# Ten of 31 depthwise-convolution taps as ScalarE products that GpSimd's transfers add up in DRAM, and one sum of weight blocks by such a transfer, in a one-core decoder-block kernel

## The chip, the cores and the metric

The kernel runs on one core of one Trainium2 chip. The metric is the device time of one execution in microseconds; lower is better. The kernel before takes 1759.72 us, the median of three runs that lie between 1759.67 and 1759.94 us.

## The reference: what is computed

One decoder block with DEPTH 1, batch 1, 1024 positions of width 1024, all in float32. Cut to what matters here:

```python
h = rms_norm(x, norm_mix_g) * (1 + sc1) + sh1                 # sh1, sc1, g1, sh2, sc2, g2 from c @ w_ada + b_ada
glu_in, qk_in, v, o_pre, if_pre, merge_pre = split(h @ w_in + b_in)
a = glu_in[..., :1024] * sigmoid(glu_in[..., 1024:])
a = causal_depthwise_conv(a, conv_dw_w, conv_dw_b)            # 31 taps: y[t] = sum_j w[j] a[t-30+j] + b, per channel
y_conv = silu(layer_norm(a)) @ w_conv_pw + b_conv_pw
q, k = split(silu(causal_depthwise_conv(qk_in, qk_conv_w, qk_conv_b)))   # 4 taps
hm = mlstm(q, k, v, gates from if_pre)                        # 4 heads of width 256, recurrent over chunks
y_mlstm = sigmoid(o_pre) * group_norm(hm)
x = x + g1 * ((sigmoid(merge_c) * y_conv + sigmoid(merge_m) * y_mlstm) @ w_out)
gt, up = split((rms_norm(x, norm_ffn_g) * (1 + sc2) + sh2) @ w_ffn_up)   # 2 x 2816 columns
out = rms_norm(x + g2 * ((silu(gt) * up) @ w_ffn_down))
```

The change touches two places: the 31-tap convolution of `a`, and the sums of blocks of `w_ffn_up` in the up projection.

## The kernel before, in words

**Numbers.** A float32 product is made of three passes of TensorE over rounded parts: high times high, high times low, low times high. So each 512 KB block of weights (tile `wraw`, 128 x 1024) is split by one ScalarE activation (`whi`, L149) and one VectorE subtraction (`wlo`, L150); `wraw`, `whi` and `wlo` have two buffers each, and the split of a block therefore waits until TensorE has done with the block before the last.

**Stages.** A prologue normalises and transposes x. Then comes the long stage that this text calls the mixing stage, from about 67 to 817 us: the input projection `w_in` in blocks of 128 columns (`wblock`, 48 matmuls of 128 x 512 at L159 and about 11 us each), with the four heads of the mLSTM between them (`mlstm`; its query, key and value blocks at L500 to L563, its recurrent steps at L593 to L690). Layer norm over the convolution, the pointwise convolution, w_out, the up projection, the down projection and the final norm follow. Activations lie with channels on partitions, 1024 positions along the free axis; eight channel tiles `ct` of 128 channels make up the width.

**The 31-tap convolution.** For each channel tile, `glu(ct)` computes two blocks; `glu_gate` makes the sigmoid (L364), `glu_post` writes tile `a` (128 x 1054, with 30 zeros in front; three buffers) and appends 31 steps to a list `bg`. Step 0 is a ScalarE activation that begins the sum `cacc` (L338), steps 1 to 30 are VectorE scalar_tensor_tensor operations on it (L340), 128 x 1024 each. After step 30 a transfer on SyncE's queue stores `cacc` in `conv_d[ct]` in DRAM. Each block of `w_in` takes steps from the list (`pump`): a block brings a credit of PUMP = 5500 and each step costs TAP = 1200, so between four and five taps go beside one block. `go` writes straight into the tile `cv` of the later layer norm where that exists already (`late["cv"]`). Behind the heads, `reload_conv()` loads all stored tiles back on SyncE's queue.

**The order of instructions.** The program is written in the order of those lists, and a list scheduler with a model of time then puts each engine's instructions into a fixed order. On the chip each engine runs its own order, one after the other, and an instruction whose wait is not yet over holds all that stand behind it.

**The up projection.** It multiplies 2 x 2 blocks by seven products instead of eight. For each of the 22 tiles f of 128 columns, `up_sums` loads the gate block g and the up block u (512 KB each, two queue entries on SyncE's queue) and makes three VectorE sums and differences of their halves (128 x 512 each): s3 (L1003), u's first half plus its second half, in place (L1004), two more (L1005, L1006). ScalarE and VectorE then split the results (L994, L995) and `up_run` does the seven products (L1054 to L1056). `up_park` does the sums of the first two tiles ahead, while w_out runs.

Of the kernel before, what the change touches and what calls it, by code (L numbers as in the profile page):

```python
# [8 lines left out]
F32 = mybir.dt.float32  # L9
F32R = mybir.dt.float32r  # L10
I32 = mybir.dt.int32
AF = mybir.ActivationFunctionType
OP = mybir.AluOpType
AX = mybir.AxisListType

S = 1024
# [4 lines left out]
FT = FF // 128  # L21
EPS = 1e-6
TAPS = 31
PUMP = 5500
TAP = 1200
LATER = 500
# [23 lines left out]
def hybrid_block(ctx: ExitStack, tc: tile.TileContext, x, c, w_ada, b_ada, norm_mix_g, w_in, b_in,  # L50
                 conv_dw_w, conv_dw_b, conv_ln_g, conv_ln_b, w_conv_pw, b_conv_pw, qk_conv_w,
                 qk_conv_b, mlstm_norm_g, w_out, norm_ffn_g, w_ffn_up, w_ffn_down, final_norm_g, out):
    nc = tc.nc
# [11 lines left out]
    def ps_mm():  # L65
        return ps.tile([128, 2, 512], F32, name="mm", bufs=2)

    def ps_a():
        return ps.tile([128, 512], F32, name="pa", bufs=1)

    def ps_n():
        return ps.tile([128, 512], F32, name="pn", bufs=1)

    def ps_c():
        return ps.tile([128, 512], F32, name="pc", bufs=2)

    bg = []
# [4 lines left out]
    def pump(ns):  # L82
        credit[0] = min(credit[0] + ns, 1e9) if bg else 0.0
        while bg and credit[0] > 0:
            cost, fn = bg.pop(0)
            at = tc.cur_priority
            tc.cur_priority = at + delay[0]
            fn()
            tc.cur_priority = at
            credit[0] -= cost  # L90
# [52 lines left out]
    def load_split(src, row0, kt, col0, hi=None, lo=None, raw=None, eng=None):  # L143
        if raw is None:
            raw = load_raw(src, row0, kt, col0)
        if hi is None:
            hi = wp.tile([128, kt, 128], F32R, name="whi", tag="whi")
            lo = wp.tile([128, kt, 128], F32R, name="wlo", tag="wlo")
        nc.scalar.activation(hi, raw, AF.Copy)  # L149
        (eng or nc.vector).tensor_sub(lo, raw, hi.bitcast(F32))  # L150
        return hi, lo
# [19 lines left out]
    def flat(t):  # L171
        return t.rearrange("p a b -> p (a b)")
# [41 lines left out]
    def bcol(col0):  # L214
        if col0 < IF0:
            return cols["b_lo"][:, col0 // 128:col0 // 128 + 1]
        i = (col0 - MC0) // 128
        return cols["b_hi"][:, i:i + 1]

    def dw_col(j, ct):  # L220
        r = j * 8 + ct
        return cols["dw0"][:, r:r + 1] if r < 128 else cols["dw1"][:, r - 128:r - 127]
# [3 lines left out]
    for q in range(2):  # L226
# [12 lines left out]
        for k in range(KT):  # L239
            p = ps_n() if k % 3 == 0 else ps_c()  # L240
# [8 lines left out]
    first = [ps_mm(), ps_mm()]  # L249
# [68 lines left out]
    cp = cvp.enter_context(tc.tile_pool(name="cp", bufs=2, side="right", reuse_waits="tile"))  # L318
    hap = ExitStack()
    ha = hap.enter_context(tc.tile_pool(name="ha", bufs=1, side="right", reuse_waits="tile"))  # L320
    hdp = ExitStack()
    hp = hdp.enter_context(tc.tile_pool(name="hp", bufs=1, side="left", reuse_waits="tile"))
    late = {}
# [8 lines left out]
    conv_d = [dram.tile([128, S], F32, name=f"conv_d{i}") for i in range(8)]  # L332
# [3 lines left out]
    def conv_tap(acc, a, j, ct):  # L336
        if j == 0:
            nc.scalar.activation(acc, a[:, 0:S], AF.Identity, scale=dw_col(0, ct), bias=cols["dw_b"][:, ct:ct + 1])  # L338
        else:
            nc.vector.scalar_tensor_tensor(acc, a[:, j:j + S], dw_col(j, ct), acc, op0=OP.mult, op1=OP.add)  # L340

    def glu_post(ct, pa, sg):
        a = cp.tile([128, TAPS - 1 + S], F32, name="a", tag="a", bufs=3)
        nc.gpsimd.memset(a[:, 0:TAPS - 1], 0.0)
        nc.vector.scalar_tensor_tensor(a[:, TAPS - 1:], flat(pa), bcol(ct * 128), sg, op0=OP.add, op1=OP.mult)
        box = []

        def go(j):
            if j == 0:
                if "cv" in late:  # L350
                    box.append(late["cv"](ct))
                else:
                    box.append(cp.tile([128, S], F32, name="cacc", tag="cacc", bufs=2))
            conv_tap(box[0], a, j, ct)
            if j == TAPS - 1 and ct not in cv:
                nc.sync.dma_start(conv_d[ct], box[0])
                done.add(ct)

        for j in range(TAPS):
            bg.append((TAP, lambda j=j: go(j)))  # L360

    def glu_gate(ct, pb):
        sg = tmp4()
        nc.scalar.activation(sg, flat(pb), AF.Sigmoid, bias=bcol(GLU_B + ct * 128))  # L364
        return sg

    cv = {}
    done = set()

    def wblock(col0, busy=PUMP, raw=None):  # L370
        w = load_split(win, 0, KT, col0, raw=raw, eng=WN if raw is not None else None)
        acc = ps_mm()
        for k in range(KT):
            mm_k(acc, k, KT, w, hh, hl)
            pump(busy / KT)
            yield
        return acc
# [138 lines left out]
    def qkv(h):  # L516
# [26 lines left out]
        def v_half(g, ws):  # L543
            acc = ps_mm()
            for i in range(4):
# [4 lines left out]
                for k in range(KT):  # L550
# [3 lines left out]
                    nc.tensor.matmul(o, hh[k][:, ts_], lo[:, k % 4, :], start=False, stop=(k == KT - 1))  # L554
                pump(PUMP / 4)
                yield
# [148 lines left out]

    def merge_conv(e, temp, busy=PUMP):
        pm = yield from wblock(MC0 + e * 128, busy)
        sg = temp()
        with tc.high_priority():
            nc.scalar.activation(sg, flat(pm), AF.Sigmoid, bias=bcol(MC0 + e * 128))  # L710
        nc.scalar.dma_start(mc_d[e], sg)
# [18 lines left out]
    for h in range(NH):  # L730
        box = []
# [17 lines left out]
    def new_cv(ct):  # L749
        cv[ct] = ap_.tile([128, S], F32, name=f"cv{ct}", tag="cv", bufs=8)  # L750
        return cv[ct]

    late["cv"] = new_cv
    def reload_conv():
        for ct in range(8):
            if ct in done and ct not in cv:
                nc.sync.dma_start(new_cv(ct), conv_d[ct])

    reload_conv()

    def t4():
        return ap_.tile([128, S], F32, name="t4b", tag="t4b", bufs=6)
# [118 lines left out]
    p = ps_a()  # L881
# [22 lines left out]
    def k4(name):  # L904
        return up_.tile([128, S], F32, name=name, tag="k4", bufs=2)
# [80 lines left out]
    def weights(kind, name):  # L986
        return wp.tile([128, KT, 128], F32 if kind == "wraw" else F32R, name=name, tag=kind)

    def up_load(f, t, col0):
        nc.sync.dma_start(t, wup[:, col0 + f * 128:col0 + (f + 1) * 128].rearrange("(k p) e -> p k e", p=128))  # L990
        return t

    def split_into(hi, lo, t):
        nc.scalar.activation(hi, t, AF.Copy)  # L994
        nc.vector.tensor_sub(lo, t, hi.bitcast(F32))  # L995
        return hi, lo

    def up_sums(f, gate=True):
        g = up_load(f, weights("wraw", "graw") if gate else k4("graw").rearrange("p (k e) -> p k e", k=KT), 0)
        u = up_load(f, k4("uraw").rearrange("p (k e) -> p k e", k=KT), FF)  # L1000
        gw = split_into(weights("whi", "gh"), weights("wlo", "gl"), g) if gate else None
        s3 = k2("s3").rearrange("p (k e) -> p k e", k=4)
        nc.vector.tensor_sub(s3, g[:, 0:4], u[:, 0:4])  # L1003
        nc.vector.tensor_add(u[:, 0:4], u[:, 0:4], u[:, 4:8])  # L1004
        nc.vector.tensor_sub(g[:, 0:4], u[:, 0:4], g[:, 0:4])  # L1005
        nc.vector.tensor_sub(g[:, 4:8], g[:, 4:8], g[:, 0:4])  # L1006
        return gw, u, g, s3
# [218 lines left out]
    for gidx, nf in enumerate(groups):  # L1226
# [4 lines left out]
        for t in range(8):  # L1231
# [3 lines left out]
            if gidx < 3:  # L1235
                p = ps_mm()
# [40 lines left out]
```

## Time and profile before

| what | value |
| --- | --- |
| three runs | 1759.67, 1759.72, 1759.94 us |
| span of the profiled execution, first to last instruction | 1757.5 us |
| what lies around the span (median less span) | 2.2 us |
| TensorE matmul busy | 1716.9 us, 98% |
| VectorE busy | 1253.3 us, 71% |
| ScalarE busy | 610.9 us, 35% |
| GpSimd busy | 72.9 us, 4% |
| mean granted TensorE clock | 0.994 |
| HBM traffic | 102 GB/s over the span |

All times are microseconds of the one core. PE is TensorE (PEld its weight loads), DVE is VectorE, ACT ScalarE, POOL GpSimd, SP SyncE; L340 is line 340 of the kernel. A row of groups gives line, engine, operation, output and inputs with their shapes, the count, then busy time and mean nanoseconds of one, then how long the engine sat idle just before them and which instruction ended that. A row of the windows gives a stretch of the span and how long each engine was busy in it. A row of the timeline gives start and duration of one instruction, with the idle time before it in brackets. A row of the transfers gives the count, the size of one and the median time from issue to landing. The profiled execution's own time is taken as its span and the 2.2 us around it, 1759.7 us, which is the median of the runs.

### The profile page before, as it was taken

Reading aid. Unit: us, or ns where it says so; the run is one execution under the profiler, and the core shown is the slowest. Engines: PE = TensorE matmul, PEld = TensorE weight load, DVE = VectorE, ACT = ScalarE, POOL = GpSimd, SP = SyncE. Lnnn points to the kernel's source line nnn. Section 1 sums busy time; section 2 is a strip of 40 time slices with the busy share of each in tenths; the row PEclk is TensorE's granted clock in tenths of the full one; section 3 lists DMA queues with packets and bytes.
Section 4 is the critical chain, followed back from the end, with each engine's and each line's share of the span. In section 5 each row is a group of like instructions: output and inputs, shape, how many; then the busy total and the mean of one; then the engine's idle time right before and its main releaser. Section 6 shows DMA issues by size and latency. Waiting matters only on the chain.

```text
span 1757.5 us, 21022 instructions
## 1 busy us (share of the span) xinstructions
PE 1716.9 (98%) x8448; PEld 1436.9 (82%) x8448; DVE 1253.3 (71%) x1652; ACT 610.9 (35%) x791; POOL 72.9 (4%) x121
## 2 busy tenths in 40 slices
PE   5999999999999999999999999999999999999998
PEld 4788888888888888888888788888888888878887
DVE  6888998996689858737689567866666665685243
ACT  6434334322533243223522366423222321232122
POOL 3100001000100000000000000000000000000000
PEclk8999999999999999999999999999999999999999
DMA  9121111111111211224497643322222222653221
GB/s 333 33 60 40 46 60 49 49 60 60 49 37 60 62 46 48 73 60 163 136 374 261 204 156 109 108 84 72 84 84 84 72 85 90 221 168 104 64 89 56
DMA packets 194712, 179.93 MB, mean 102 GB/s; under 512 B 7463, under 2 KB 166711, under 8 KB 194615
## 3 DMA queue, kind: packets, MB, share of 16 engines
q1 hardware_dynamic: 177367, 146.61, 26.8%
q10 hardware_dynamic: 17248, 31.99, 5.0%
q8 instruction: 66, 1.08, 0.3%
q14 instruction: 31, 0.25, 0.0%
HBM read 146.06 MB, written 32.51 MB: 102 GB/s over the span
## 4 chain that ended last, share of the span: by engine, by line
PE 90%; DVE 4%; DMA 3%; issue 1%; ACT 1%; POOL 0%; SPq 0%; POOLq 0%; DVEq 0%; ACTq 0%
PE mm L159 39%; PE mm L1054 5%; PE mm L1055 5%; PE mm L1056 4%; PE mm L552 2%; PE mm L1240 2%; PE mm L1239 2%; PE mm L1241 2%; PE mm L553 2%; PE mm L554 2%; PE pc L1054 1%; DVE macc L268 1%; PE pc L1056 1%; PE pc L1055 1%; PE pa L1056 1%
## 5 line engine op out<-in xcount | busy, mean ns | idle before, releaser
L340 DVE SCALAR_TENSOR_TENSOR cacc<-a,col,cacc 128x1024 f32<-128x1024 f32 x240 | 307.3, 1286 | 4.1 <-ACT cacc L338 1.4
L159 PE MATMUL mm<-hh,whi 128*128 128x512 f32 x864 | 272.8, 392 | 0.8 <-ACT t L364 0.8
L159 PE MATMUL mm<-hl,whi 128*128 128x512 f32 x864 | 271.0, 392 | 0.0
L159 PE MATMUL mm<-hh,wlo 128*128 128x512 f32 x864 | 270.6, 391 | 0.0
L159 PEld LDWEIGHTS mm<-hh,whi 128*128 128x128 f32 x864 | 161.1, 188 | 32.8 <-ACT t L364 1.2
L159 PEld LDWEIGHTS mm<-hh,wlo 128*128 128x128 f32 x864 | 161.3, 188 | 32.3
L159 PEld LDWEIGHTS mm<-hl,whi 128*128 128x128 f32 x864 | 160.5, 188 | 30.9 <-issue 0.2
L149 ACT ACTIVATE whi<-wraw 128x1024 fp32r<-128x1024 f32 x62 | 65.8, 1062 | 228.7 <-PE mm L159 178.5
L150 DVE TENSOR_TENSOR wlo<-wraw,whi 128x1024 fp32r<-128x1024 f32 x60 | 73.2, 1220 | 26.1 <-ACT whi L149 26.0
L552 PE MATMUL mm<-whi,hh 128*128 128x256 f32 x256 | 76.2, 298 | 0.0
L1054 PE MATMUL mm<-Bh,gh 128*128 128x512 f32 (+1 forms) x192 | 71.6, 375 | 1.5 <-ACT gh L994 1.0
L553 PE MATMUL mm<-whi,hl 128*128 128x256 f32 x256 | 72.5, 283 | 0.0
L1055 PE MATMUL mm<-Bl,gh 128*128 128x512 f32 (+1 forms) x192 | 71.5, 373 | 0.6 <-DVE Bl L976 0.6
L554 PE MATMUL mm<-wlo,hh 128*128 128x256 f32 x256 | 71.8, 283 | 0.0
L1056 PE MATMUL mm<-Bh,gl 128*128 128x512 f32 (+1 forms) x192 | 71.2, 372 | 0.0
L505 DVE SCALAR_TENSOR_TENSOR cacc<-qkraw,col,cacc 128x1024 f32<-128x1024 f32 x48 | 61.5, 1280 | 6.7 <-ACT cacc L503 6.0
L1243 DVE TENSOR_TENSOR x<-x,mm 128x1024 f32<-128x1024 f32 x24 | 29.3, 1219 | 51.1 <-PE mm L1241 47.0
L1119 ACT ACTIVATE whi<-wraw 128x512 fp32r<-128x512 f32 (+2 forms) x32 | 25.3, 790 | 110.6 <-PE mm L1241 72.9
L552 PEld LDWEIGHTS mm<-whi,hh 128*128 128x128 f32 x256 | 48.8, 191 | 4.1
L1240 PE MATMUL mm<-fa,wlo 128*128 128x512 f32 x128 | 50.1, 392 | 1.0 <-DVE wlo L1120 0.9
L1239 PE MATMUL mm<-fa,whi 128*128 128x512 f32 x128 | 50.0, 390 | 0.9 <-DVE cu L1082 0.9
L1241 PE MATMUL mm<-fa,whi 128*128 128x512 f32 x128 | 49.9, 390 | 0.0
(442 smaller groups left out, 3898.0 us busy)
## 6 DMA issues: line engine op xcount, KB each, us to landing
wraw<-in_w_in_dram SPq DMA_DIRECT2D x64, 512.0 KB, 4.2
awt<-in_w_ada_dram SPq DMA_DIRECT2D x32, 512.0 KB, 8.1
graw<-in_w_ffn_up_dram SPq DMA_DIRECT2D x24, 512.0 KB, 3.8
uraw<-in_w_ffn_up_dram SPq DMA_DIRECT2D x22, 512.0 KB, 4.7
draw<-in_w_ffn_down_dram SPq DMA_DIRECT2D x22, 512.0 KB, 4.4
act_d<-cg ACTq DMA_DIRECT2D x38, 256.0 KB, 2.2
wad<-in_w_ada_dram SPq DMA_DIRECT2D x16, 512.0 KB, 10.2
wraw<-in_w_out_dram SPq DMA_DIRECT2D x16, 512.0 KB, 4.3
```

The source lines that it names most:

```text
L150: (eng or nc.vector).tensor_sub(lo, raw, hi.bitcast(F32))
L159: nc.tensor.matmul(flat(acc)[:, a:b], lhs[:, k, :], rhs[k][:, a:b], start=(first and k == 0), stop=(last and k == kt - 1))
L340: nc.vector.scalar_tensor_tensor(acc, a[:, j:j + S], dw_col(j, ct), acc, op0=OP.mult, op1=OP.add)
L552: nc.tensor.matmul(o, hh[k][:, ts_], hi[:, k % 4, :], start=False, stop=False)
L553: nc.tensor.matmul(o, hl[k][:, ts_], hi[:, k % 4, :], start=False, stop=False)
L554: nc.tensor.matmul(o, hh[k][:, ts_], lo[:, k % 4, :], start=False, stop=(k == KT - 1))
L1054: nc.tensor.matmul(o, a, rh, start=(k == 0), stop=False)
L1055: nc.tensor.matmul(o, a, rl, start=False, stop=False)
L1056: nc.tensor.matmul(o, b, rh, start=False, stop=(k == 3))
L1239: nc.tensor.matmul(o, hi[:, i, :], his[i][:, a:b], start=(i == 0), stop=False)
L1240: nc.tensor.matmul(o, lo[:, i, :], his[i][:, a:b], start=False, stop=False)
L1241: nc.tensor.matmul(o, hi[:, i, :], los[i][:, a:b], start=False, stop=(i == nf - 1))
```

## The change

Per channel tile, taps 0 to 20 stay as they were (one on ScalarE, 20 on VectorE). Taps 21 to 30 become ScalarE activations that write the product of one tap into a tile `tapp` (two buffers). The first of the ten products is stored in `conv_d[ct]` by a transfer on SyncE's queue; the other nine are added to it there by transfers of GpSimd's queue that add instead of copying (`accum_op`), and so is `cacc` at the end. Each of these ten reads and writes the same 512 KB of DRAM, so each waits for the one before it. Tile `a` has two buffers instead of three. The direct way into `cv` and the first `reload_conv()` are gone; the last one loads all eight tiles. In `up_sums` the addition of L1004 becomes a transfer of GpSimd's queue that adds u's second half to its first in SBUF (256 KB), 22 times.

```diff
+SENT = 10
...
     def glu_post(ct, pa, sg):
-        a = cp.tile([128, TAPS - 1 + S], F32, name="a", tag="a", bufs=3)
+        a = cp.tile([128, TAPS - 1 + S], F32, name="a", tag="a", bufs=2)
...
         def go(j):
             if j == 0:
-                if "cv" in late:
-                    box.append(late["cv"](ct))
-                else:
-                    box.append(cp.tile([128, S], F32, name="cacc", tag="cacc", bufs=2))
+                box.append(cp.tile([128, S], F32, name="cacc", tag="cacc", bufs=2))
             conv_tap(box[0], a, j, ct)
-            if j == TAPS - 1 and ct not in cv:
-                nc.sync.dma_start(conv_d[ct], box[0])
-                done.add(ct)
-
-        for j in range(TAPS):
+
+        def send(j, first):
+            p = ha.tile([128, S], F32, name="tapp", tag="tapp", bufs=2)
+            nc.scalar.activation(p, a[:, j:j + S], AF.Copy, scale=dw_col(j, ct))
+            if first:
+                nc.sync.dma_start(conv_d[ct], p)
+            else:
+                nc.gpsimd.dma_start(conv_d[ct], p, accum_op=OP.add)
+
+        def last():
+            nc.gpsimd.dma_start(conv_d[ct], box[0], accum_op=OP.add)
+            done.add(ct)
+
+        near, far = range(TAPS - SENT), range(TAPS - SENT, TAPS)
+        for n, j in enumerate(near):
             bg.append((TAP, lambda j=j: go(j)))
+            if n % 2 == 0 and n // 2 < SENT:
+                bg.append((0, lambda j=far[n // 2], n=n: send(j, n == 0)))
+        bg.append((0, last))
...
-    late["cv"] = new_cv
...
-    reload_conv()
...
-        nc.vector.tensor_add(u[:, 0:4], u[:, 0:4], u[:, 4:8])
+        nc.gpsimd.dma_start(u[:, 0:4], u[:, 4:8], accum_op=OP.add)
```

The change moves instructions on ScalarE and GpSimd above all. In the rows below a name carries the number of its buffer, `[waits ...]` names what the instruction waits for: `DMASWn` a transfer of GpSimd's queue, `DMAHWn` one of the other queues, `Pool` GpSimd. Lines of the kernel after stand some eleven higher than those of before (L538 is L549).

The first place is ScalarE around the first two key blocks and the first value block of head 0, in the kernel before:

```order
L149 ACTIVATE whi_1054<-wraw_1052 128x1024 [waits DMAHW0_49,PE_49]
L506 ACT_TABLE_LOAD
L506 ACTIVATE cacc_832<-cacc_832,col2_525 128x1024 [waits DVE_49]
L500 ACTIVATE qkraw_930<-mm_848,col5_513 128x1024 [waits PE_49,Activation_49]
L509 ACTIVATE kh_838<-cacc_832 128x1024 [waits Activation_49]
L503 ACTIVATE cacc_933<-qkraw_930,col2_525 128x1024 [waits DVE_49,Pool_49]
L538 ACTIVATE whi_1126<-wraw_1125 128x1024 [waits DMAHW1_49,PE_49]
```

And the same place in the kernel after:

```order
L356 ACTIVATE tapp_1289<-a_704,col4_521 128x1024 [waits DMASW4_49]
L150 ACTIVATE whi_1089<-wraw_1087 128x1024 [waits DMAHW1_49,PE_49]
L511 ACTIVATE qkraw_957<-mm_869,col5_513 128x1024 [waits PE_49]
L514 ACTIVATE cacc_960<-qkraw_957,col2_525 128x1024 [waits DMASW1_49,Activation_49,Pool_49]
L339 ACTIVATE cacc_1024<-a_704,col2_525,col3_517 128x1024 [waits DVE_49]
L356 ACTIVATE tapp_1347<-a_704,col4_521 128x1024 [waits DMASW5_49]
L356 ACTIVATE tapp_1402<-a_704,col4_521 128x1024 [waits DMASW6_49]
L356 ACTIVATE tapp_1459<-a_704,col4_521 128x1024 [waits DMASW7_49,Activation_49]
L517 ACTIVATE cacc_960<-cacc_960,col2_525 128x1024 [waits DVE_49]
L549 ACTIVATE whi_1167<-wraw_1166 128x1024 [waits DMAHW3_49,PE_49]
```

The sends of channel tile 1 (`a_704`) have come between the splits of weight blocks: whi_1167, the first of the value block (whi_1126 before), now stands behind tapp_1459, whose wait for DMASW7 is the wait for the tile's sixth adding transfer. Ahead of that stand the nine adding transfers of tile 0 and its `cacc`, one behind the other.

The second place is ScalarE near the end of channel tile 3 (`a_2000`), before the queries and keys of head 1. The kernel before has there:

```order
L149 ACTIVATE whi_2286<-wraw_2284 128x1024 [waits DMAHW0_49,PE_49]
L500 ACTIVATE qkraw_2198<-mm_2145,col5_513 128x1024 [waits PE_49,Activation_49]
L624 ACTIVATE kwh_1788<-pa_1790,wsc_694 128x256 [waits PE_49]
L624 ACTIVATE kwh_1788<-pa_1790,wsc_694 128x256 [waits DVE_49,PE_49]
L503 ACTIVATE cacc_2201<-qkraw_2198,col2_525 128x1024 [waits DVE_49,DMAHW3_49,Activation_49,Pool_49]
```

The kernel after has there:

```order
L150 ACTIVATE whi_2304<-wraw_2302 128x1024 [waits DMAHW7_49,PE_49]
L511 ACTIVATE qkraw_2209<-mm_2149,col5_513 128x1024 [waits PE_49]
L635 ACTIVATE kwh_1856<-pa_1858,wsc_709 128x256 [waits PE_49]
L356 ACTIVATE tapp_2582<-a_2000,col4_521 128x1024 [waits DMASW2_49,Activation_49]
L514 ACTIVATE cacc_2212<-qkraw_2209,col2_525 128x1024 [waits Activation_49]
L339 ACTIVATE cacc_2265<-a_2000,col2_525,col3_517 128x1024 [waits DMASW6_49]
L356 ACTIVATE tapp_2640<-a_2000,col4_521 128x1024 [waits DMASW3_49]
L635 ACTIVATE kwh_1856<-pa_1858,wsc_709 128x256 [waits DVE_49,PE_49]
```

The second kwh_1856, a factor of the recurrent step that TensorE takes next (kwh_1788 before), has moved behind tapp_2640, which waits for the sixth adding transfer of tile 3; ten of tile 2 go ahead of that.

The third place is GpSimd's queue from the last adding transfers of tile 0 on. The kernel before has only small fills there:

```order
L416 MEMSET wif_703 128x1024 [waits PE_49]
L499 MEMSET qkraw_930 128x3 [waits DVE_49,Activation_49,Pool_49]
L344 MEMSET a_1926 128x30 [waits DVE_49]
L499 MEMSET qkraw_1039 128x3 [waits DVE_49,Activation_49]
L499 MEMSET qkraw_1112 128x3 [waits DVE_49,Activation_49]
```

The kernel after has:

```order
L360 DMA conv_d0_541<-tapp_940 128x1024 [waits DMASW6_49,Activation_49]
L360 DMA conv_d0_541<-tapp_989 128x1024 [waits DMASW7_49,Activation_49]
L345 MEMSET a_1701 128x30 [waits DVE_49]
L363 DMA conv_d0_541<-cacc_581 128x1024 [waits DMASW0_49]
L360 DMA conv_d1_542<-tapp_1107 128x1024 [waits DMAHW2_49,Activation_49]
L360 DMA conv_d1_542<-tapp_1136 128x1024 [waits DMASW2_49,Activation_49]
L360 DMA conv_d1_542<-tapp_1204 128x1024 [waits DMASW3_49,Activation_49]
L510 MEMSET qkraw_957 128x3 [waits DVE_49,Pool_49]
L360 DMA conv_d1_542<-tapp_1259 128x1024 [waits DMASW4_49,Activation_49]
```

Each adding transfer waits for the one before it and for its ScalarE product, and holds GpSimd's queue while it waits; the fills stand between them.

## The prediction

> **What bounds the kernel now.** I read the shares of the page first, then windows of the span by stage, then TensorE's waits.
>
> ```profile
> span 1757.5 us, 21022 instructions
> PE 1716.9 (98%) x8448; PEld 1436.9 (82%) x8448; DVE 1253.3 (71%) x1652; ACT 610.9 (35%) x791; POOL 72.9 (4%) x121
> ```
>
> TensorE leaves 1757.5 - 1716.9 = 40.6 us free in the whole run; no other engine is near full. That is the most that any change to the other engines can win. The windows (start and end, length, then busy us of each engine, clock, DMA share, GB/s) say where those 40.6 us lie:
>
> ```profile
> 88.00:836.00 748.00, 748.00 (x4007) 641.62 (x4006) 592.58 (x757) 263.45 (x309) 40.68 (x79) 1.00 0.20 61
> 968.00:1056.00 88.00, 84.46 (x385) 69.55 (x384) 57.01 (x84) 44.69 (x66) 2.19 (x4) 0.98 0.54 180
> 1056.00:1144.00 88.00, 83.67 (x532) 74.17 (x531) 69.64 (x125) 47.40 (x74) 2.45 (x4) 1.00 0.34 108
> 1144.00:1496.00 352.00, 352.00 (x1520) 285.35 (x1519) 223.01 (x301) 96.52 (x122) 0.00 (x0) 1.00 0.27 83
> 1496.00:1584.00 88.00, 86.08 (x376) 70.21 (x375) 67.08 (x68) 28.42 (x35) 0.00 (x0) 1.00 0.55 188
> ```
>
> From 88 to 836 us, where the convolution runs, TensorE is busy 748.00 of 748.00 us. VectorE, which the change relieves there, works 592.58 of the 748, and TensorE does not wait for it. The same holds in the steady up projection: 352.00 of 352.00. Only the seams around the parks (968 to 1144) and the start of the down projection leave 3.54 + 4.33 + 1.92 = 9.8 us. TensorE's list of waits, line waited for with total, times and longest, agrees:
>
> ```profile
> PE pa L946 <- ACT whi L940: 3.5, 1, 3.5
> PE mm L159 <- ACT t L364: 0.8, 1, 0.8
> ```
>
> The first is the largest wait behind the prologue; the second is the only one of the mixing stage, once and 0.8 us. So the kernel is bound by TensorE, and the question about the change is whether the weights and factors still arrive in time.
>
> **What the change removes.** The groups give the price of a tap, of the ScalarE operation most like a send, and of the sum in the up projection:
>
> ```profile
> L340 DVE SCALAR_TENSOR_TENSOR cacc<-a,col,cacc 128x1024 f32<-128x1024 f32 x240 | 307.3, 1286 | 4.1 <-ACT cacc L338 1.4
> L503 ACT ACTIVATE cacc<-qkraw,col 128x1024 f32<-128x1024 f32 x16 | 18.5, 1154 | 2.4 <-DVE pl L455 1.4 <-DMA conv_d<-cacc 0.3
> L1004 DVE TENSOR_TENSOR uraw<-uraw 128x512 f32<-128x512 f32 x22 | 15.1, 684 | 0.0
> ```
>
> VectorE loses 80 x 1.286 = 102.9 us of taps and 22 x 0.684 = 15.1 us of sums. ScalarE gains 80 x 1.154 = 92 us, which it has room for by time (263.45 busy of 748). None of this reaches the end while TensorE is full: the 102.9 us are worth 0.
>
> **What it adds: a chain of transfers.** Per channel tile there are ten adding transfers of 512 KB, each after the one before. Call T the time from one to the next. Because `tapp` has two buffers, send k waits for the transfer of send k-2, so ScalarE, whose order is fixed, is bound to that chain, with the splits of the weight blocks queued behind. Nothing in the trace before issues a transfer from GpSimd or adds in one, so T has to be bounded by the nearest rows (count, KB each, us to landing):
>
> ```profile
> wraw<-in_w_in_dram SPq DMA_DIRECT2D x64, 512.0 KB, 4.2
> graw<-in_w_ffn_up_dram SPq DMA_DIRECT2D x24, 512.0 KB, 3.8
> act_d<-cg ACTq DMA_DIRECT2D x38, 256.0 KB, 2.2
> xt<-in_x_dram SPq DMA_DIRECT2D x4, 1024.0 KB, 5.0
> yg_d<-t ACTq DMA_DIRECT2D x8, 512.0 KB, 3.4
> ```
>
> Lower end: an addition costs no more than the plain store of the same 512 KB, 3.4 us. Upper end: it costs a store and a load one after the other, 3.4 + 4.2 = 7.6 us. Between them: store 3.4, plus 1.2 for moving 512 KB more (the 1024 KB load less the 512 KB load, 5.0 - 3.8), plus 0.6 for GpSimd's issue and the wait between two, which is my guess: T = 5.2 us. The nearest row is the store, so I stay nearer to that end.
>
> Now the deadlines. In ScalarE's timeline before (start, duration):
>
> ```profile
> 69.24 1.25 ACT L338 ACTIVATE cacc<-a,col,col 128x1024 f32<-128x1024 f32 x1 [1.41 <-DVE a L345]
> ...
> 119.41 1.06 ACT L149 ACTIVATE whi<-wraw 128x1024 fp32r<-128x1024 f32 x1 [6.09 <-PE mm L159]
> 130.29 1.07 ACT L538 ACTIVATE whi<-wraw 128x1024 fp32r<-128x1024 f32 x1 [2.90 <-PE mm L159]
> 131.39 1.15 ACT L506 ACTIVATE cacc<-cacc,col 128x1024 f32<-128x1024 f32 x1
> ```
>
> ```profile
> L150 DVE TENSOR_TENSOR wlo<-wraw,whi 128x1024 fp32r<-128x1024 f32 x60 | 73.2, 1220 | 26.1 <-ACT whi L149 26.0
> ```
>
> *Tiles 0 and 1.* The first store can land at 69.24 + 1.25 + 1.15 + 3.4, about 75.0; I take 75.5. The value block's split (130.29 before, released by the end of a block of TensorE) comes after the change behind the send that waits for 9 + 1 + 6 = 16 links of the chain. Blocks end 130.29 - 119.41 = 10.9 us apart, so TensorE wants these weights at about 141.3. Behind the sixteenth link stand a send 1.15, the L506 operation 1.15, the split 1.06 and 1.22: 4.6 us. Hence 75.5 + 16 T + 4.6 = 141.3 gives T = 3.85 as the limit, and the stall beyond it is 16 (T - 3.85): at 5.2, 21.6 us.
>
> ```profile
> 194.50 1.24 ACT L338 ACTIVATE cacc<-a,col,col 128x1024 f32<-128x1024 f32 x1 [1.20 <-DVE a L345]
> ...
> 271.57 0.48 ACT L624 ACTIVATE kwh<-pa,wsc 128x256 fp32r<-128x256 f32 x1 [5.30 <-PE pa L621]
> ```
>
> *Tiles 2 and 3.* The store of tile 2 can land at 194.50 + 1.24 + 1.15 + 3.4 = 200.3. The second half of the third kwh (271.57 before), which TensorE's recurrent step uses, comes behind the same 16 links and a send: 16 T + 1.15 = 71.3, T = 4.38, stall 16 (T - 4.38) = 13.1 us.
>
> ```profile
> 344.44 1.25 ACT L338 ACTIVATE cacc<-a,col,col 128x1024 f32<-128x1024 f32 x1 [1.19 <-DVE a L345]
> ...
> 377.39 0.48 ACT L624 ACTIVATE kwh<-pa,wsc 128x256 fp32r<-128x256 f32 x1 [4.11 <-PE pa L621]
> ...
> 527.94 1.24 ACT L338 ACTIVATE cacc<-a,col,col 128x1024 f32<-128x1024 f32 x1 [0.26 <-DVE a L345]
> ```
>
> *Tiles 4 to 7.* These have a stage each to themselves. Tile 4's store lands at about 350.2, and the kwh of 377.39 comes behind six links and a send: 6 T + 1.15 = 27.2, T = 4.34, stall 6 (T - 4.34) = 5.2 us. Tile 6 (tap 0 at 527.94) has the same steps behind it, 5.2 us. For tiles 5 and 7 I count nothing at 5.2 and half of tile 4's beyond about 5.5, an estimate.
>
> *GpSimd's and SyncE's queues.* The denominators of the mLSTM (L676 to L680) now queue on GpSimd behind the waiting transfers. For head 0 they began at 244.0 (row below) and come behind eight links of tile 2, 200.3 + 8 T = 241.9 at 5.2: hidden, with 2 us to spare; beyond T = 5.5 they are late by 8 us per us of T, in the same time in which ScalarE is late already. Weight loads on SyncE stand behind the first store of a tile, which waits only for a ScalarE product; the split they feed is queued behind that product anyway. Price 0 for both.
>
> ```profile
> 244.00 1.20 POOL L676 TENSOR_TENSOR den<-den 128x4 f32<-128x4 f32 x1 [24.75 <-DVE den L675]
> ```
>
> *The dropped reload* costs nothing that I can see: before, all eight loads of conv_d are issued together at the end of the stage (787.45), and so they are now.
>
> ```profile
> 787.45 4.97 SPq L757 DMA_DIRECT2D cv<-conv_d  x8
> ```
>
> *The up projection.* One sum of one period in the timeline, and its reader:
>
> ```profile
> 1219.80 0.68 DVE L1004 TENSOR_TENSOR uraw<-uraw 128x512 f32<-128x512 f32 x1
> ...
> 1223.22 1.06 ACT L994 ACTIVATE uh<-uraw 128x1024 fp32r<-128x1024 f32 x1 [3.21 <-PE pn L1055]
> ```
>
> The split of u waits until 1223.22 for TensorE anyway. The transfer can start once s3 has read u, about 1219.3, so up to 3.9 us are hidden; 256 KB stored take 2.2, and with T's ratio 5.2/3.4 it is 3.4 us. Price 0 in the 20 steady tiles; at the two parks, where VectorE runs without a gap, up to 4 us each way. I enter 0.
>
> **The sum.** 21.6 + 13.1 + 5.2 + 5.2 = 45.1 us on the profiled execution's 1759.7 (span 1757.5 and 2.2 around it, the median of the runs): 1804.8 us, say 1805.
>
> The Trainium skill speaks for a smaller T: in "DMA: Bandwidth & Descriptors", section "Anatomy of one DMA — SWDGE (gpsimd) path", it fits a GpSimd transfer as 2.0 us plus bytes over 436,000 per us, 3.2 us for 512 KB as an estimate, and gives no own figure for adding. No trace here shows it; the sum by it would be 0.
>
> **The rivals.**
>
> *The additions are as quick as stores (not slower).* If T stays at or under 3.85, every deadline above is met, and the stalls are 0: 1760. For it: the store takes 3.4, and the adding happens where the data pass. Against: the destination has to be read too, 512 KB more, and a fixed order of ScalarE leaves 0.4 us per link. The fit of the Trainium skill above would mean this case. Chance 0.17.
>
> *The seams win (faster).* On top of a hidden chain, the 15.1 us that VectorE loses near the parks could close the 3.54 + 4.33 us of 968 to 1144: 1752. Against: 3.5 of those wait for ScalarE's whi L940, not for VectorE, and the transfer's result comes later than the sum did. Chance 0.05.
>
> *The addition is a load, then a store.* T of 6.2 to 7.6. At 6.6: 44.0 + 35.5 + 13.6 + 13.6 + 14 (tiles 5 and 7) = 121, 1880; at 7.6 over 170, 1930 and more. For it: reading the destination cannot overlap its own writing in full. Against: by the rows 512 KB more cost 1.2 us, so some 2.2 of the store's 3.4 us are no data and would not be paid twice. Chance 0.18.
>
> **How the numbers follow.** The forecast, T between about 4.1 and 6.2, has 0.60. What a measurement of this kernel can tell from no change is about 0.2%, 3.5 us, which T passes just above 4.05. So slower 0.60 + 0.18 = 0.78, same 0.17, faster 0.05. The range runs from 1758, which takes in the hidden chain, to 1880, T = 6.6; outside lie the seams' gain and the upper part of the third rival, together under 0.2.
>
> **What would show it.** In the profile after, the window 88 to 836, stretched, should miss about 45 us of TensorE, two thirds of them before about 290 us, with waits of TensorE for whi, wlo and kwh, and ScalarE idle ahead of L356, released by transfers from `tapp` into `conv_d`. Two successive additions should start about 5.2 us apart. The up projection should keep its period. The forecast is wrong if T is under 4 (no stall), if ScalarE's sends never wait, or if TensorE waits in the up projection instead.

## The result, and the profile after

The kernel after takes 1904.09 us (1902.95 to 1907.08, four runs) against 1759.83 for the kernel before: a ratio of 1.082, with a 95% interval of 1.0806 to 1.0834. It is slower by 144 us, where 45 were forecast and 1880 was the upper end of the range. First the page's opening lines of the kernel after:

```profile
span 1902.1 us, 21309 instructions
PE 1761.4 (93%) x8448; PEld 1462.9 (77%) x8448; DVE 1144.2 (60%) x1550; ACT 691.5 (36%) x869; POOL 152.2 (8%) x223
```

Two things stand in them. TensorE now leaves 1902.1 - 1761.4 = 140.7 us free, where it left 40.6: 100.1 us more of waiting. And it is busy 44.5 us longer with the same 8448 matmuls. The two make the 144.6 us by which the span grew. The windows of the kernel after, in the columns of the prediction, say where:

```profile
88.00:220.00 132.00, 104.12 (x502) 85.98 (x501) 78.37 (x105) 52.82 (x54) 15.78 (x24) 0.87 0.58 108
220.00:396.00 176.00, 145.26 (x741) 122.33 (x739) 103.18 (x138) 72.34 (x82) 27.47 (x41) 0.93 0.49 96
396.00:528.00 132.00, 120.52 (x613) 102.44 (x613) 64.83 (x103) 45.30 (x57) 12.16 (x19) 0.95 0.42 88
528.00:660.00 132.00, 122.27 (x655) 104.32 (x654) 81.29 (x96) 57.54 (x60) 16.41 (x27) 0.97 0.44 90
660.00:836.00 176.00, 157.19 (x797) 133.19 (x796) 100.69 (x125) 67.19 (x72) 22.19 (x36) 0.94 0.50 101
836.00:968.00 132.00, 132.00 (x671) 112.19 (x670) 63.24 (x110) 38.91 (x52) 3.96 (x11) 1.00 0.29 92
```

From 88 to 836 us TensorE was never idle before; now it is idle for 27.9 + 30.7 + 11.5 + 9.7 + 18.8 = 98.6 us of it, nearly all that was added, and only as long as there are channel tiles to send. The column before the last two is the granted clock. It was 1.00 and is 0.87 to 0.97 in the same windows. That mean also counts idle time, so the cost to the work is read from the stretches themselves: in the mixing stage the trace has 18 stretches at 0.50, 99.0 us long, in which TensorE is busy for 73.7 us. At 1.00 that work would have taken half as long, so 37 of the 44.5 us are the lower clock. The other 7 or 8 the clock does not explain. Part of them may be how busy time is counted: the last matmul before a gap counts with 0.39 us, where in a stream one starts every 0.23, and there are 62 gaps where there were 25, so some 6 us by an estimate from these figures.

Who makes TensorE wait, and what ScalarE waits for, from the lists of waits of the kernel after:

```profile
PE mm L160 <- ACT qkraw L511: 16.8, 3, 6.6
PE pn L584 <- ACT sch L620: 11.2, 3, 7.6
PE pc L584 <- ACT kwh L635: 11.1, 4, 4.3
PE pc L584 <- ACT Ch L674: 10.3, 4, 5.4
PE pa L700 <- DVE num L693: 9.7, 2, 5.1
...
PE pa L488 <- DVE uT L481: 7.6, 1, 7.6
...
ACT tapp L356 <- DMA conv_d<-tapp: 239.7, 65, 6.4
```

ScalarE sits 239.7 us ahead of sends, for a transfer to land. What TensorE lacks is what is queued behind the sends on ScalarE: the copies of TensorE's results out of its accumulators (qkraw), factors of the recurrent steps (sch, kwh, Ch), and by way of ScalarE's share in the gates also uT. The list of transfers and a stretch of GpSimd's timeline give the length of a link, the time from one adding transfer to the next (the prediction's T):

```profile
conv_d<-tapp POOLq DMA_DIRECT2D x72, 512.0 KB, 5.4
uraw<-uraw POOLq DMA_DIRECT2D x22, 256.0 KB, 3.3
```

```profile
92.75 0.89 POOL L360 DMA_DIRECT2D conv_d<-tapp  x1 [5.14 <-DMA conv_d<-tapp]
98.66 0.87 POOL L360 DMA_DIRECT2D conv_d<-tapp  x1 [5.03 <-DMA conv_d<-tapp]
104.43 0.86 POOL L360 DMA_DIRECT2D conv_d<-tapp  x1 [4.90 <-DMA conv_d<-tapp]
110.30 0.86 POOL L360 DMA_DIRECT2D conv_d<-tapp  x1 [5.00 <-DMA conv_d<-tapp]
```

From 92.75 to 110.30 are three links: 5.85 each (over the first eight of tile 0, from 74.81 to 122.43, 5.95). Most links lie between 5.7 and 6.1; some, mainly where one tile's chain meets the next, take 6.3 to 9. The forecast had 5.2.

### The profile page after: what moved, and what is told of

It is laid out like the page before. It is cut to its first block, busy times and chain, and to the rows that moved or that the text cites. A ratio compares the mean times of both kernels' runs of the same rounds, so it can differ in the third digit from the quotient of the medians.

```text
span 1902.1 us, 21309 instructions
## 1 busy us (share of the span) xinstructions
PE 1761.4 (93%) x8448; PEld 1462.9 (77%) x8448; DVE 1144.2 (60%) x1550; ACT 691.5 (36%) x869; POOL 152.2 (8%) x223
## 4 chain that ended last, share of the span: by engine, by line
PE 49%; DVE 3%; DMA 3%; issue 1%; ACT 1%; SPq 0%; POOLq 0%; POOL 0%; ACTq 0%; DVEq 0%
PE mm L160 12%; PE mm L1062 4%; PE mm L1063 4%; PE mm L1064 4%; PE mm L1248 2%; PE mm L1247 2%; PE mm L1249 2%; PE pc L1062 1%; PE pc L1064 1%; PE pc L1063 1%; PE pa L1062 1%; PE pa L1064 1%; PE pa L1063 1%; PE pn L1063 1%; PE pn L1064 1%
## 5 line engine op out<-in xcount | busy, mean ns | idle before, releaser
L160 PE MATMUL mm<-hh,whi 128*128 128x512 f32 x864 | 280.7, 403 | 20.4 <-ACT qkraw L511 16.8
L160 PE MATMUL mm<-hl,whi 128*128 128x512 f32 x864 | 278.1, 400 | 0.0
L160 PE MATMUL mm<-hh,wlo 128*128 128x512 f32 x864 | 275.9, 399 | 0.0
L160 PEld LDWEIGHTS mm<-hh,whi 128*128 128x128 f32 x864 | 165.8, 195 | 54.9 <-ACT qkraw L511 18.0
L341 DVE SCALAR_TENSOR_TENSOR cacc<-a,col,cacc 128x1024 f32<-128x1024 f32 x160 | 204.7, 1280 | 3.3 <-ACT cacc L339 1.4
L160 PEld LDWEIGHTS mm<-hh,wlo 128*128 128x128 f32 x864 | 165.9, 193 | 34.2
L160 PEld LDWEIGHTS mm<-hl,whi 128*128 128x128 f32 x864 | 166.0, 194 | 33.3
L356 ACT ACTIVATE tapp<-a,col 128x1024 f32<-128x1024 f32 x80 | 91.3, 1149 | 239.7 <-DMA conv_d<-tapp 239.7
L360 POOL DMA_DIRECT2D conv_d<-tapp x72 | 63.2, 877 | 390.5 <-DMA conv_d<-tapp 336.0
L1012 POOL DMA_DIRECT2D uraw<-uraw x22 | 19.2, 873 | 527.1 <-DVE cu L1091 315.2
```

The source lines that it names most:

```text
L160: nc.tensor.matmul(flat(acc)[:, a:b], lhs[:, k, :], rhs[k][:, a:b], start=(first and k == 0), stop=(last and k == kt - 1))
L356: nc.scalar.activation(p, a[:, j:j + S], AF.Copy, scale=dw_col(j, ct))
L360: nc.gpsimd.dma_start(conv_d[ct], p, accum_op=OP.add)
```

## The experiments

The theory, A: the chain of adding transfers holds ScalarE's fixed order, and the work queued behind comes late. K: a long gap also lowers TensorE's clock. Rivals: the up projection has its part (B), ScalarE's added work and new order (C), the bytes of the transfers (D), every link costs its part whatever the deadlines are (E), GpSimd's queue is what starves TensorE (G).

**Each half of the change alone.** Before with only the sum of the up projection replaced:

```diff
-        nc.vector.tensor_add(u[:, 0:4], u[:, 0:4], u[:, 4:8])
+        nc.gpsimd.dma_start(u[:, 0:4], u[:, 4:8], accum_op=OP.add)
```

> The up projection's sum by transfer alone, the convolution as before. Theory A (the chain of adding transfers in the mixing stage makes all of the 144 us): 1760, within 2 us of before, since TensorE's waits around the parks are about as long after the change as before (8.7 against 7.9 us). Rival B (the transfers of the up projection have a part in it): 1765 or more, with waits of TensorE for uh, ul or s in the steady tiles. The transfer itself: 3.3 us from issue to landing, as after.

Measured: 1762.89 us (1761.46 to 1763.6, eleven runs) against 1759.44, ratio 1.0016 (1.0007 to 1.0025). Neither number was quite met: 3 us, and no wait for uh, ul or s in the steady tiles. Where the 3 us are: the timeline's split of u stands at 1145.36 us before and at 1147.90 here, at the first tiles behind the parks, and at 1456.82 and 1459.32 sixteen tiles later, so the steady period is the same 19.46 us. They are lost while the parks run beside w_out; there is a new wait of TensorE in the list, with 3.41 us of half clock behind it that cost 1.6, while the wait for L940 is 1.0 shorter (2.5 for 3.5):

```profile
PE mm L948 <- DVE wlo L941: 2.4, 1, 2.4
```

The convolution's change alone, the other half:

> The convolution's change alone, the up projection's sum on VectorE as before. Theory A (all in the chain of adding transfers): 1903 to 1905, as after. Rival B (the up projection has a part in it): 1898 or less.

Measured: 1889.71 us (1887.85 to 1892.62). That is 14 us under the kernel after, where the half above costs 3. The link was shorter too, 5.1 us to landing instead of 5.4, so both were run again on one chip.

> The kernel after once more, beside the convolution's change alone on the same chip: the two differed by 14 us on two occasions, where the up projection's change alone cost 3. If the link is a little shorter or longer from chip to chip (5.95 us there, 5.7 in the convolution's change alone), the two now lie within 5 us of each other, with the same link. If the 14 us belong to the kernels, they come again: 1904 against 1890.

> The convolution's change alone once more, beside the kernel after on the same chip: within 5 us of it if the length of a link varies from chip to chip, 14 us under it if the difference belongs to the kernels.

Measured: 1894.02 us (1892.87 to 1895.57) for the kernel after and 1890.42 (1889.21 to 1891.61) for the convolution alone, 3.6 us apart, both with 5.1 us to landing and 5.7 to 5.8 us a link in tile 0. On another chip the kernel after took 1896.52, again with 5.1. So the first result's other 10 us came with a longer link in that measurement, 5.95 us for 5.72 in tile 0: over the 16 + 16 + 6 + 6 = 44 links that the prediction prices that makes 10. The halves add up (131 + 3 against 135), and B is out but for its 3 us. Comparisons below are with 1894 to 1897, the kernel after where a link is 5.7 to 5.8.

**The adding.** As after, with every order of every engine as it is, but the transfer copies:

```diff
-                nc.gpsimd.dma_start(conv_d[ct], p, accum_op=OP.add)
+                nc.gpsimd.dma_start(conv_d[ct], p)
```

> As after, but the nine transfers of GpSimd's queue per channel tile copy instead of adding; the same 512 KB of DRAM is written each time, so each still waits for the one before it, and no order of any engine changes. (The sum of the taps is left out: nine of the ten products are overwritten.) Theory A (the time of a link decides): the link falls from 5.95 us to some 4.2 (0.9 of issue, 3.4 as a store lands, less than that if the two overlap), stalls 16 x (4.2 - 3.85) = 6 us in tiles 0 and 1 and little else: 1760 to 1775. Rival C (the new order of ScalarE and its 92 us of products, or the waits themselves, whatever a link takes): 1860 or more. Rival D (the bytes of the transfers crowd out the weight loads): the bytes written stay, so at least half of the 144 us stays, over 1830.

Measured: 1787.75 us, ratio 1.0166 (1.0152 to 1.018). GpSimd's timeline, then the list of transfers:

```profile
81.80 0.53 POOL L360 DMA_DIRECT2D conv_d<-tapp  x1 [1.96 <-DMA conv_d<-tapp]
85.22 0.53 POOL L360 DMA_DIRECT2D conv_d<-tapp  x1 [2.90 <-DMA conv_d<-tapp]
88.62 0.53 POOL L360 DMA_DIRECT2D conv_d<-tapp  x1 [2.87 <-DMA conv_d<-tapp]
```

```profile
conv_d<-tapp POOLq DMA_DIRECT2D x72, 512.0 KB, 2.9
```

A link is 3.4 us instead of 5.7, 2.9 to landing instead of 5.1, and 107 us of the 135 are gone; the traces have the same instructions in the same order on ScalarE, VectorE, GpSimd and TensorE. C would have kept most of it. So would D as it was put, but the copies also drop the reads that an addition makes; against D speaks the kernel after itself, where between 88 and 836 us no engine waits for a block of weights to be loaded. The 28 that stay are more than the 0 to 15 that A expected; the next two runs take them apart.

Copies, each into a DRAM tile of its own, so that no transfer waits for another:

```diff
-                nc.gpsimd.dma_start(conv_d[ct], p, accum_op=OP.add)
+                nc.gpsimd.dma_start(part_d[ct][m], p)
```

> As after, but each of the nine products of GpSimd's queue goes by a copy into a DRAM tile of its own, so no transfer waits for another; the last, of the VectorE sum, still adds. (The sum of the taps is left out.) ScalarE still makes 80 products, and each waits for the copy two before it to free the buffer. Theory A: no chain, no stall, 1758 to 1763. Rival C (ScalarE's 92 us and the new order): 1830 or more. Rival D (bytes): 1830 or more.

Measured: 1778.62 us, ratio 1.0107 (1.0093 to 1.0121). Without the chain 19 us stay, 9 fewer than with the copies in a chain. The two runs differ in more than the chain: the list scheduler gave this one another order, with the sends earlier (the 20th send stands behind 89 other ScalarE instructions, and behind 95 in the kernel after and with the chained copies). So that a chain of 3.4 us a link, under the prediction's limit of 3.85, still costs 9, and that the deadlines leave less room than it worked out, is likely but not shown by this pair.

Products alone, no transfer, VectorE's sum stored as before:

```diff
-            if first:
-                nc.sync.dma_start(conv_d[ct], p)
-            else:
-                nc.gpsimd.dma_start(conv_d[ct], p, accum_op=OP.add)
...
-            nc.gpsimd.dma_start(conv_d[ct], box[0], accum_op=OP.add)
+            nc.sync.dma_start(conv_d[ct], box[0])
```

> The convolution's change without its transfers: ScalarE still makes the 80 products, VectorE still has 80 taps fewer, the buffers are as in after, but no product leaves the chip's core, and the VectorE sum is stored as before (the ten taps are missing from the output). The up projection is as before. Theory A: 92 us of ScalarE work beside TensorE cost nothing, 1758 to 1762. Rival C (the 17 us that stay with the copies into tiles of their own, the up projection's 3 taken off, are ScalarE's work and its new order): 1770 to 1777.

Measured: 1763.84 us (1762.61 to 1765.57, eleven runs) against 1759.89, ratio 1.0021 (1.0012 to 1.003). ScalarE does all 80 products, waits 1.1 us ahead of them, and VectorE's 102.9 us are gone:

```profile
L356 ACT ACTIVATE tapp<-a,col 128x1024 f32<-128x1024 f32 x80 | 85.7, 1139 | 1.1 <-DVE a L346 1.1
```

It gains nothing and loses 4 us. So the added work costs 4 here, in an order that the scheduler made for it, and the relief of VectorE is worth nothing. The order of the kernel after was not run without transfers; the chained copies, which have it, lose 28 in all, so C makes at most 28 of the 135. If the runs are taken as alike in order, of the 19 us with the copies apart 4 are this and 3 the up projection's; the other 12 come with copies that only free a buffer, and what makes them was not tried further.

**Two chains.** Products by turns into two DRAM tiles, VectorE adds the second when it is loaded back:

```diff
+            to = (conv_d, side_d)[m % 2][ct]
+            if m < 2:
+                nc.sync.dma_start(to, p)
+            else:
+                nc.gpsimd.dma_start(to, p, accum_op=OP.add)
...
+            side = t4()
+            nc.sync.dma_start(side, side_d[ct])
+            nc.vector.tensor_add(cv[ct], cv[ct], side)
```

> As after, but the products go by turns into two DRAM tiles per channel tile, so that a transfer adds while the one after it is already under way and waits only for the one before the last; the first product of each tile is stored, VectorE adds the second tile when they are loaded back. The whole of the computation is done. Theory A1 (a link is mostly waiting, and two overlap): a send comes every 3 us or so, under the 3.85 that the deadlines leave, 1775 to 1790, as with the copies. Theory A2 (the adding itself has a rate, 512 KB in 4 us or more by the 256 KB that take 3.3 us in the up projection, and two share it): a send every 4.5 to 6 us, 1800 to 1904.

Measured: 1832.8 us (1830.05 to 1835.05), ratio 1.0416 (1.0401 to 1.0432). GpSimd's timeline:

```profile
82.47 0.86 POOL L362 DMA_DIRECT2D conv_d<-tapp  x1 [3.01 <-ACT tapp L357]
86.69 0.89 POOL L362 DMA_DIRECT2D side_d<-tapp  x1 [3.35 <-ACT tapp L357]
89.17 0.88 POOL L362 DMA_DIRECT2D conv_d<-tapp  x1 [1.60 <-ACT tapp L357]
93.27 0.86 POOL L362 DMA_DIRECT2D side_d<-tapp  x1 [3.23 <-ACT tapp L357]
95.91 0.86 POOL L362 DMA_DIRECT2D conv_d<-tapp  x1 [1.78 <-ACT tapp L357]
```

Two sends come every 6.7 us, 3.4 each: two additions do overlap, as A1 says, and in this stretch the pace is that of the copies. But the time is A2's. Half of the loss goes, not all of it. One new wait of 6.1 us belongs to the added tile loads behind the stage. For the rest the run leaves open why this pace costs more here than with the copies; the order is another one here too, with the 20th send behind 89 other ScalarE instructions instead of 95.

**Fewer sends.** SENT = 4 and SENT = 7 instead of 10:

> As after with four taps per channel tile sent instead of ten: three adding transfers and the one of the VectorE sum, so four links where there were ten. Theory A (links against a deadline): tiles 0 and 1 have 3 + 1 + 2 links and 35 us for 66 us of room; no stall from the chain, 1760 to 1775. Rival E (every link costs its part, 144 us over 80 links): 1760 + 0.4 x 144 = 1818.

Measured: 1767.63 us, ratio 1.0048 (1.0033 to 1.0063). A's number; E's 1818 is far off. TensorE's idle time in the mixing stage is down to single waits of under 0.8 us. With 32 of 80 links, 8 us stay, of which 3 are the up projection's.

> As after with seven taps per channel tile sent. Theory A (links against a deadline): in tiles 0 and 1 the split of the second key block stands behind 8 links, 75 + 8 x 5.8 = 121.4 us and 3.4 us of work, against about 119.5: some 5 us late; the value block behind 11 links, 139 us, about in time; in all 1770 to 1795. Rival E (every link costs its part): 1760 + 0.7 x 134 to 144 = 1854 to 1861.

Measured: 1833.62 us (1829.85 to 1835.97), ratio 1.0415 (1.04 to 1.0429). This misses both: A's 1770 to 1795 by 40, E's by 20. The list of waits of TensorE names what A's sum for the weights left out:

```profile
PE pa L700 <- DVE num L693: 9.6, 2, 7.5
...
PE pa L476 <- DVE z L470: 7.1, 1, 7.1
PE mm L160 <- ACT qkraw L511: 6.8, 2, 3.7
```

Not the splits, of which I had worked out two, but the gates (z needs ScalarE's exponential of L458, which stands behind a send and runs at 125.8 us, where it ran at 113.1 before) and the denominators come late. From 4 to 7 to 10 sends the loss goes 8, 74, 135: little up to a point, then about 21 us for each send more per channel tile. That there is a threshold is right; it comes earlier than the weights' deadlines say.

**GpSimd's queue.** As after, but the fills and the denominators are VectorE's work:

```diff
-            nc.gpsimd.tensor_mul(w2, r, r)
+            nc.vector.tensor_mul(w2, r, r)
...
-            rsqrt(sd, w2)
+            nc.vector.reciprocal(sd, w2)
```

> As after, but what else stood in GpSimd's queue between the adding transfers of the mixing stage is done by VectorE: the fills and the denominators of the mLSTM (whose power of -1/2 becomes a reciprocal, so the scale of the heads is another); only the eight AFFINE_SELECTs of the masks stay. ScalarE's sends and the chain are as in after. Theory A (ScalarE's order is what the chain holds up): TensorE's two waits for num, 9.7 us with some 5 us of lower clock behind them, go, the rest stays: 10 to 20 us under after on the same chip. Rival G (GpSimd's queue, held by the waiting transfers, is what starves the recurrent steps): 40 us or more under after.

> The kernel after on the same chip, to compare with: 1890 to 1906, with the link between 5.7 and 6.0 us.

Measured on one chip: 1890.79 us (1889.04 to 1895.43) against 1896.52 (1892.71 to 1899.84). 6 us, hardly clear of the spread of the runs, less than A's 10 to 20 and far from G's 40. The two waits for num, 8.6 us in the kernel after on this chip, are one of 4.5 now, and others grew in their place, the wait for kwh from 8.5 to 17.4:

```profile
PE pc L584 <- ACT kwh L635: 17.4, 4, 8.2
...
PE pa L700 <- DVE num L693: 4.5, 1, 4.5
```

So it is not what else stood in GpSimd's queue that starves TensorE: with that gone, TensorE is idle for 130.3 us, and for 129.9 in the kernel after on the same chip. GpSimd's queue is a second victim, and mostly in the same time.

**The clock.** In the kernel after, windows of 2 us around one gap (start and end, length, busy us of the engines, clock, DMA share, GB/s):

```profile
312.00:314.00 2.00, 2.00 (x12) 1.62 (x10) 0.00 (x0) 0.00 (x0) 0.00 (x0) 1.00 0.62 121
314.00:316.00 2.00, 0.11 (x1) 0.00 (x0) 0.00 (x0) 1.15 (x1) 0.86 (x1) 1.00 0.00 0
316.00:318.00 2.00, 0.00 (x0) 0.00 (x0) 0.00 (x0) 0.00 (x0) 0.00 (x0) 1.00 0.98 125
318.00:320.00 2.00, 0.00 (x0) 0.00 (x0) 0.00 (x0) 0.00 (x0) 0.00 (x0) 0.66 0.70 137
320.00:322.00 2.00, 0.33 (x1) 0.33 (x2) 0.35 (x1) 1.56 (x2) 0.88 (x1) 0.50 0.00 0
322.00:324.00 2.00, 2.00 (x7) 1.61 (x7) 0.21 (x1) 0.00 (x0) 0.00 (x0) 0.50 1.08 158
324.00:326.00 2.00, 2.00 (x7) 1.61 (x6) 0.00 (x0) 0.03 (x1) 0.00 (x0) 0.63 0.54 104
326.00:328.00 2.00, 2.00 (x10) 1.62 (x9) 0.00 (x0) 2.00 (x3) 0.87 (x1) 1.00 0.23 14
```

TensorE stops at about 314.1 and goes on at 321.7. The clock stays at 1.00 until some 4.5 us into the gap, then goes to 0.50, and stays there until about 325.5, through 3.8 us of work: 7 matmuls in 2 us instead of 10 to 12. To take the transfers out of this, the kernel before, with none of the change, had gate blocks held up on GpSimd:

```diff
+HOLD = {5: 6, 8: 8, 11: 10, 14: 12, 17: 14}
...
+        for _ in range(HOLD.get(f, 0) if gate else 0):
+            nc.gpsimd.tensor_scalar(g, g, 1.0, None, op0=OP.mult)
```

> The kernel before, with nothing of the change, but five of the gate blocks of the up projection are held up on the idle GpSimd by 6, 8, 10, 12 and 14 multiplications by one in place, so that TensorE runs dry five times, for longer each time. What is measured is the granted clock around each gap. Theory K (a long gap lowers the clock, as after 288 and 314 us in the kernel after, where it goes to 0.50 some 4 us into the gap and stays there for 4 to 5 us of the work that follows): gaps over 4 us cost their length and some 2 us more each, shorter ones their length alone. Rival: the lower clock of the kernel after comes with the transfers or the stage; then it stays at 1.00 here and the time added is the sum of the gaps.

Measured: 1766.86 us against 1759.89, ratio 1.0038 (1.0024 to 1.0051). Three of the holds were hidden by the loads' lead; the longest two made gaps of 2.39 and 3.48 us, which end at 1355.49 and 1418.80. Behind them, windows of 2 us of this run:

```profile
1354.00:1356.00 2.00, 0.51 (x2) 0.47 (x3) 2.00 (x4) 0.96 (x2) 0.00 (x0) 1.00 0.00 0
1356.00:1358.00 2.00, 2.00 (x7) 1.57 (x7) 2.00 (x5) 1.33 (x2) 0.00 (x0) 0.68 0.68 201
1358.00:1360.00 2.00, 2.00 (x6) 1.58 (x5) 2.00 (x3) 0.68 (x1) 0.00 (x0) 0.50 0.25 70
1360.00:1362.00 2.00, 2.00 (x9) 1.57 (x9) 2.00 (x4) 0.00 (x0) 0.00 (x0) 0.96 0.25 72
...
1418.00:1420.00 2.00, 1.21 (x3) 1.01 (x4) 1.79 (x3) 2.00 (x3) 0.00 (x0) 0.54 0.54 192
1420.00:1422.00 2.00, 2.00 (x7) 1.52 (x6) 2.00 (x3) 1.16 (x2) 0.00 (x0) 0.50 0.04 8
1422.00:1424.00 2.00, 2.00 (x6) 1.60 (x5) 2.00 (x4) 0.63 (x1) 0.00 (x0) 0.50 0.00 0
1424.00:1426.00 2.00, 2.00 (x8) 1.56 (x7) 2.00 (x5) 0.77 (x2) 0.00 (x0) 0.75 0.29 73
```

The clock falls to 0.50 in a kernel without a single transfer of GpSimd's queue, so K stands and its rival falls: missing from 1.00 are 2 x (0.32 + 0.50 + 0.04) = 1.7 us behind the first gap and 2 x (0.46 + 0.50 + 0.50 + 0.25) = 3.4 at the second, of which 0.3 lie in the gap itself. K's guess of 4 us as the limit was wrong: 2.39 us were enough. The gaps and the lower clock are 5.9 + 4.8 = 10.7 us; the span grew by 9.4, the median by 7.0.

What decides is not the gap's length alone. In all the traces the clock changes only on a grid of 3.41 us, and a stretch at 0.50 lasts one, two or three steps of it (3.41, 6.83 or 10.24 us; the last one is cut short by the end of the trace). From 60 us on, all 139 steps at 1.00 in which TensorE was idle for more than 0.57 of the step were followed by one at 0.50, and no step with less than 0.37 was; between the two both happen. So a gap of 2.46 us in the kernel after (from 1167.38 us), which falls half into one step and half into the next, brought no lower clock, and one of 1.62 us (from 110.30), which lies nearly whole in one step and fills 0.43 of it, did.

The Trainium skill has the mechanism, in "TensorE: Matmul & The Clock Gate", section "Part 1: The HAM clock gate": half the clock after an idle window of about 3.4 us, full again after a busy one. The half clock agrees (0.50), and so do losses of 1.7 us, which are 3.4 at half clock; that TensorE must be idle for all of 3.4 us does not.

## Why the prediction was wrong, step by step

- **TensorE bounds the kernel, and relief of VectorE is worth nothing: right.** The products alone, with 102.9 us of VectorE's work gone, gain nothing (1763.84 against 1759.89). The second rival's 15.1 us were misread: they are the sums of all 22 tiles, and only two of them, 1.4 us, stand at the parks.
- **The mechanism, ScalarE's order bound to a chain of adding transfers, with what TensorE needs queued behind: right.** 239.7 us of ScalarE's waits, and 107 of 135 us gone when the same transfers copy. But the waits that the prediction named, for whi, wlo and kwh, are a quarter of the 98.6 us (4.6 + 2.8, 6.4 and 11.1); TensorE waits longer for qkraw, sch, Ch and the gates, whose deadlines it did not work out.
- **"T = 5.2 us": too small, 5.95.** A copy of GpSimd's queue took 2.9 us to landing, less than the store's 3.4; the adding put 2.2 to 2.5 on top, where I had 1.2 for the bytes read; 0.5 lies between landing and the next issue. With 5.95 in the prediction's own formulas the stalls are 33.6 + 25.1 + 9.7 + 9.7 = 78 and up to 10 for tiles 5 and 7 at half of tile 4's, together 88. Measured idle time is 27.9 in the window of tiles 0 and 1, 30.7 in that of tiles 2 and 3, 40.0 in those of tiles 4 to 7, 98.6 in all. So with the right T the formulas give the first four tiles together (58.7 against 58.6; the two misses of 6 us cancel, which is luck), and tiles 4 to 7, at 29, were priced too low. (The limit of 3.85 is 3.83 by the prediction's own figures, which makes 0.4 us.)
- **"The sum: 21.6 + 13.1 + 5.2 + 5.2 = 45.1 us": the step that put the time outside the range.** It priced a stall at its own length and the clock behind it at nothing. In the mixing stage 18 stretches of half clock came with the gaps and cost the work 1.5 to 3.7 us each, 37 us in all; with the 7 or 8 us that stay unexplained, that is the 44.5 us by which TensorE is busy longer. Without that term even the measured chain would have given 1759.7 + 99, 1859, inside the range; with it, no T near 5.9 stays there. By size the two failures are alike: T and the deadlines left out make the idle time 98.6 instead of 45, and the clock does the rest.
- **"Price 0 for both" queues: nearly right in effect, wrong in kind.** TensorE did wait 9.7 us for denominators behind transfers, but taking them out of the queue saved 6 us, hardly clear of the spread. SyncE's share no run takes apart.
- **The up projection at 0: 3 us, at the parks**, where the prediction had put a bound of 4 each way; the steady tiles hid the transfer (3.3 us, 3.4 forecast).
- **The rivals.** Additions as quick as stores did not come: 5.1 to 5.4 us. The fit from the Trainium skill's page "DMA: Bandwidth & Descriptors", section "Anatomy of one DMA — SWDGE (gpsimd) path", 3.2 us for 512 KB as an estimate, is near the copies here (2.9 to 3.1) and says nothing of an addition. The third rival gave about the right time, 1880 to 1930, for the wrong reason: single links were that long, but most took 5.7 to 6.1, not the 6.2 to 7.6 that it asks for.

No version ran faster than the kernel before: four sends take 1767.63, the products alone 1763.84.

## What to carry to other kernels

Before work is moved off an engine, look in the stage's window whether anyone waits for it; here TensorE was busy 748 of 748 us, and there was nothing to win. A chain of transfers with few buffers ties the engine that fills them to the transfers' pace: count links against the first deadline of everything queued behind, not only of the weights. And where TensorE is the bound, a gap can cost more than its length: look at the granted clock in windows of 2 us behind each gap.

## What the runs showed of the hardware

- A transfer of 512 KB from SBUF to DRAM on GpSimd's queue took 2.9 to 3.1 us to landing as a copy and 5.1 to 5.4 as an addition; issuing it held GpSimd 0.53 and 0.87 us. An addition of 256 KB within SBUF took 3.3 us. Two additions into different tiles overlapped: one every 3.4 us in the stretch shown.
- The same addition differed between measurements of the same kernel: 5.72 us a link in one, 5.95 in another, and the kernel after with it by 10 us, while the median of the kernel before stayed within 0.5. That it is the chip that differs is not shown.
- The granted clock of TensorE went to 0.50 and back only on a grid of 3.41 us, for 3.41, 6.83 or 10.24 us at a time. From 60 us on it fell after every step in which TensorE was idle for more than 0.57 of it, and after none with less than 0.37. A gap of 2.39 us was enough, and one of 1.62 that lay nearly whole in one step; one of 2.46 that two steps shared was not.
